# An S5 scan inside a matmul stream: two blocks encoded and two decoded in one visit of TensorE, and two of each block's sums on GpSimd

## The chip, the cores and the metric

The kernel runs on one core of a Trainium2 chip. The metric is the device time of one execution in microseconds; lower is better. The core's engines are TensorE (PE in the profile, with its weight loads as PEld), VectorE (DVE), ScalarE (ACT), GpSimd (POOL) and SyncE (SP, which here only issues DMAs). Each takes its instructions in the order in which the built program holds them, and waits on semaphores for the others.

## The reference

Two layers of a decoder trunk over 256 positions of width 2048. The first joins a Mamba-2 mixer and an attention; the second, which the change touches, is an S5 mixer: a projection to u and a gate, 128 groups of 16 channels that each drive a complex diagonal state of 64, then GELU, a GLU, the gate and an output projection.

```python
def s5_ssm(u, lam_re, lam_im, log_dt, b_re, b_im, c_re, c_im, d_skip):
    ...
    lam_bar = jnp.exp(lam * dt)
    b_bar = ((lam_bar - 1.0) / lam)[..., None] * lax.complex(b_re.astype(f32), b_im.astype(f32))
    ...
    def step(h, u_blk):
        bu = jnp.einsum('gnm,blgm->blgn', b_bar, u_blk.astype(jnp.complex64))
        bu = bu.at[:, 0].add(lam_bar * h)
        a = jnp.broadcast_to(lam_bar, bu.shape)
        _, hs = lax.associative_scan(_linear_recurrence, (a, bu), axis=1)
        y = jnp.einsum('gmn,blgn->blgm', c_mat, hs).real
        return hs[:, -1], y
    ...

def s5_mixer(x, w_in, ..., w_glu, w_out):
    u, gate = jnp.split(x @ w_in, 2, axis=-1)
    y = jax.nn.gelu(s5_ssm(u, ...))
    ga, gb = jnp.split(y @ w_glu, 2, axis=-1)
    y = ga * jax.nn.sigmoid(gb)
    return (y * jax.nn.silu(gate)) @ w_out
```

## The kernel before

**The stream of weights.** All projections are cut into units: 128x1024 blocks of weights, each loaded by SyncE into a buffer `raw` (L361), rounded by ScalarE to a high half `wh` (L367), and reduced by VectorE to the rest `wl` (L372). `wh`, `wl` and `raw` have four buffers each, and `split_to` (L328) prepares a unit three units ahead. TensorE multiplies high by high, high by low and low by high. In the products of kind x (L425) a unit is 12 matmuls of 512 columns; in the wide ones (L481, L484) it is 8 of 512 and 8 of 256.

**The scan between the units.** The second layer's scan is done in 16 blocks `b` of 8 groups, while TensorE works on the input projection's later products. `ssm(b)` defines the parts of a block: `load` brings its weights `wt` (896 KB, L1578) by a DMA of GpSimd's queue; `u_load` brings its input `um` for two blocks in four DMAs (L1558, L1559); `table` fills `rt` on GpSimd (L1585, L1586); `enc` is 16 matmuls of 64x64 into the PSUM tile `enc` (L1595); `rec1` turns that by cos and sin on VectorE, two products (L1605) and two sums (L1612, L1613); `rec2` is the recurrence itself, two scans along positions (L1620), two products that turn back (L1607) and two sums (L1622, L1623) into `gt`; `dec` is 24 matmuls of 64x64 from `gt` and `um` into the PSUM tile `dec` (L1636, L1640); `act` is a GELU on ScalarE (L1644) and four DMAs of 32 KB of ScalarE's queue (L1648, L1649). Each small matmul is two records in the profile. `y_load` brings four blocks' y back (L1662), and `y_split` cuts it in high and low halves (L1672, L1673). `wt` has four buffers, `gt`, `p1`, `p2`, `rt` and `ys` two, the PSUM tiles `enc` and `dec` one.

**What sets the order.** `at(t, f)` puts a part on step t, and the steps are a queue `back` that `pump` empties evenly over the units of seven products and eight units more. A scheduler then lays out each engine's instructions by its own timeline at build time; `tc.issue_after` ties an instruction behind another on its engine. Encode of block b stands on step 2b+1 (0 for the first), its decode on 2b+5: each visit of TensorE to the small matmuls decodes one block and encodes the block two further on. The first two visits only encode and the last two only decode, 18 visits in all.

Of the kernel before, what the change touches and what calls it, by code (L numbers as in the profile page):

```python
# [16 lines left out]
P = 128  # L17
# [6 lines left out]
HU = KT // HK  # L24
ALPHA = 4.0 ** 0.25
NKEEP = 6
NEND = 448
# [162 lines left out]
def trunk(tc, io, out):  # L190
# [8 lines left out]
    with ExitStack() as top:  # L199
# [1310 lines left out]
        with ExitStack() as l1:  # L1510
# [49 lines left out]

            steps = {}

            def at(t, f):
                steps.setdefault(t, []).append(f)

            ysd = {}

            def ssm(b):
# [4 lines left out]
                def load():  # L1573
                    wt = d["w"] = w1("wt", [P, 1792], 4)
                    with ExitStack() as pin:
                        if b:
                            pin.enter_context(tc.issue_after((after[b - 1] if b > 2 else after["u"]).ins))
                        nc.gpsimd.dma_start(wt, wb[b])  # L1578
# [9 lines left out]
                def enc():  # L1588
                    px = d["x"] = sp.tile([P, 2, 512], F32, tag="enc", name=nm("enc"))
                    wt, u = d["w"], um[b // 2]  # L1590
                    for q in range(2):
                        for r in range(2):
                            for e, i, at in tiles:
                                a = 2 * q + e
                                T.matmul(px[64 * at : 64 * at + 64, i, r * 128 + q * 64 : r * 128 + q * 64 + 64],  # L1595
                                         wt[64 * i : 64 * i + 64, a * P + 64 * r : a * P + 64 * r + 64],
                                         u[64 * i : 64 * i + 64, 4 * b2 + a, :], start=True, stop=True)

                def turned(src):
                    p1, p2 = w1("p1", [P, 2, 256]), w1("p2", [P, 2, 256])  # L1600
                    for p, t in ((p1, d["cos"]), (p2, d["sin"])):
                        if src is None:
                            t4 = t.rearrange("p r (i n) -> p r i n", i=2)
                            sv = d["x"][:, :, 0:256].rearrange("p i (r n) -> p r i n", r=2)
                            V.tensor_tensor(p.rearrange("p r (i n) -> p r i n", i=2), sv, t4, op=OP.mult)  # L1605
# [4 lines left out]
                def rec1():  # L1610
                    p1, p2 = turned(None)
                    V.tensor_tensor(p1[:, 0], p1[:, 0], p2[:, 1], op=OP.add)  # L1612
                    V.tensor_tensor(p1[:, 1], p1[:, 1], p2[:, 0], op=OP.subtract)  # L1613
                    d["p"] = p1

                def rec2():
# [5 lines left out]
                    V.tensor_tensor(gt[:, 0], p1[:, 0], p2[:, 1], op=OP.subtract)  # L1622
                    V.scalar_tensor_tensor(gt[:, 1], p1[:, 1], -1.0, p2[:, 0], op0=OP.mult, op1=OP.subtract)  # L1623

                def dec():
                    wt, u, gt = d["w"], um[b // 2], d["g"]
                    py = d["y"] = sp.tile([P, 2, 512], F32, tag="dec", name=nm("dec"))
                    for q in range(2):
                        for part in range(3):
                            for e, i, at in tiles:  # L1630
                                a = 2 * q + e
                                rows = slice(64 * at, 64 * at + 64)
                                o = py[64 * e : 64 * e + 64, at, q * 64 : q * 64 + 64]
                                if part == 0:
                                    rhs = u[rows, 8 + 2 * b2 + q, :] if e else u[rows, 4 * b2 + a, :]
                                    T.matmul(o, wt[rows, 1024 + 64 * a : 1088 + 64 * a], rhs, start=True, stop=False)  # L1636
                                else:
                                    k = 512 + 256 * (part - 1) + 64 * (2 * i + q)
                                    n = 64 * (2 * i + q)
                                    T.matmul(o[:, 1:64], wt[rows, k : k + 64], gt[rows, part - 1, n : n + 63], start=False, stop=part == 2)  # L1640

                def act():
                    ys = w1("ys", [P, 2, 2, 64])
                    A.activation(ys, d["y"][:, :, 0:128].rearrange("p i (q c) -> p i q c", c=64), AF.Gelu_apprx_tanh)  # L1644
                    dst = yd[j][16 * h : 16 * h + 16].rearrange("(i q e) a c -> e a i q c", i=2, e=2)
# [4 lines left out]

                t = 2 * b + min(b, 1)
                at(2 * b + 6, act)
                at(2 * b + 5, dec)
                at(t + 2, rec2)
                at(t + 1, rec1)
                at(t, enc)
                at(t - 1, table)
                at(t - 2, load)

# [30 lines left out]

            at(36, scanned)
            sg1 = wk.tile([P, 2, D], F32, tag="sg1", bufs=1, name="sg1")
# [263 lines left out]
```

## Time and profile before

| | |
|---|---|
| time, median of 3 runs | 1300.84 us (1300.39 to 1301.18) |
| the profiled execution: time, span | 1300.75 us, 1299.0 us |
| first encode, last decode, start | 878.3 us, 1042.4 us |
| granted TensorE clock | 0.998 of full speed, mean |

The span runs from the first to the last instruction; the 1.75 us around it are the launch. The scan lies between 878 and 1043 us. In the rows of a timeline the start comes first, then the duration, engine, line, operation and tiles; neighbours on an engine overlap at their edges, so what one costs in a full row is the distance from its start to the next start.

### The profile page before, as it was taken

What the parts mean: (1) busy time and instruction counts of PE and PEld (TensorE: products, weight loads), DVE (VectorE), ACT (ScalarE), POOL (GpSimd) and SP (SyncE); (2) the same over time, 40 slices, a digit from 0 to 9 for tenths busy, and PEclk for the clock granted to TensorE, in tenths of its full rate; (3) what the DMA queues carried; (4) which work ended last, traced back from release to release, by engine and by line L of the source; (5) the groups of instructions that cost most, each with busy time, mean ns of one, the idle gap of its engine ahead of it and who ended that gap; (6) DMA issues with size and microseconds to landing.
All of it is one profiled execution on the core that took longest, in us unless ns stands there. A gap on an engine that the chain in (4) does not pass through costs nothing.

```text
span 1299.0 us, 21556 instructions
## 1 busy us (share of the span) xinstructions
PE 1292.0 (99%) x7939; PEld 1091.1 (84%) x7939; DVE 1036.1 (80%) x1726; ACT 738.5 (57%) x1000; POOL 316.5 (24%) x617
## 2 busy tenths in 40 slices
PE   9999999999999999999999999999999999999998
PEld 9988888888888888888888888888888888888886
DVE  6678988996898887777777777858989859988665
ACT  5557668974644654554575555354345557766441
POOL 0033678888880000000000110023232001110000
PEclk9999999999999999999999999999999999999999
DMA  8556567666567667757759978479989789887762
GB/s 316 180 164 203 186 230 232 220 197 196 194 202 264 211 202 239 234 184 222 245 177 290 294 197 290 161 232 319 326 288 325 244 310 245 216 248 230 261 211 81
DMA packets 100094, 300.90 MB, mean 232 GB/s; under 512 B 19378, under 2 KB 29570, under 8 KB 99476
## 3 DMA queue, kind: packets, MB, share of 16 engines
q1 hardware_dynamic: 74356, 239.81, 54.7%
q0 software_dynamic: 11232, 46.18, 13.3%
q10 hardware_dynamic: 14400, 13.54, 3.2%
q8 instruction: 62, 1.02, 0.3%
q14 instruction: 44, 0.36, 0.1%
HBM read 276.93 MB, written 21.00 MB: 229 GB/s over the span
## 4 chain that ended last, share of the span: by engine, by line
PE 99%; DMA 1%; SPq 0%; ACT 0%; DVE 0%; issue 0%
PE main L425 54%; PE main L481 17%; PE main L484 9%; PE main L526 7%; PE main L448 3%; PE aux L631 2%; PE aux L979 1%; PE enc L1595 1%; PE aux L1085 1%; PE dec L1640 1%; PE aux L1204 1%; PE aux L1172 1%; DMA raw<-in_wi 1%; PE dec L1636 0%; PE turn L631 0%; PE aux L1171 0%
## 5 line engine op out<-in xcount | busy, mean ns | idle before, releaser
L372 DVE TENSOR_TENSOR wl<-raw,wh 128x1024 fp32r<-128x1024 f32 x400 | 493.6, 1239 | 185.0 <-ACT wh L367 176.0
L367 ACT ACTIVATE wh<-raw 128x1024 fp32r<-128x1024 f32 x400 | 421.2, 1058 | 367.0 <-PE main L425 184.4
L425 PE MATMUL main<-wh,A 128*128 128x512 f32 x1216 | 392.4, 394 | 0.0
L425 PEld LDWEIGHTS main<-wh,A 128*128 128x128 f32 x1216 | 228.0, 188 | 47.1 <-issue 0.3
L425 PE MATMUL main<-wh,C 128*128 128x512 f32 x832 | 265.2, 393 | 0.0
L425 PE MATMUL main<-wl,A 128*128 128x512 f32 x608 | 238.2, 392 | 0.0
L481 PE MATMUL main<-A,wh 128*128 128x512 f32 x768 | 199.4, 395 | 0.0
L425 PEld LDWEIGHTS main<-wh,C 128*128 128x128 f32 x832 | 155.9, 188 | 33.3
L425 PE MATMUL main<-wl,C 128*128 128x512 f32 x416 | 162.6, 391 | 0.0
L481 PEld LDWEIGHTS main<-A,wh 128*128 128x128 f32 x768 | 136.0, 189 | 23.1 <-issue 0.3
L425 PEld LDWEIGHTS main<-wl,A 128*128 128x128 f32 x608 | 114.3, 188 | 22.5
L484 PEld LDWEIGHTS main<-A,wl 128*128 128x128 f32 x768 | 108.8, 190 | 10.4
L484 PE MATMUL main<-A,wl 128*128 128x256 f32 x768 | 112.2, 282 | 0.0
L903 POOL TENSOR_TENSOR c<-c 128x8 f32<-128x8 f32 (+2 forms) x192 | 100.0, 538 | 26.5 <-DMA wb<-c 18.7
L324 POOL DMA_DIRECT2D block<-in_wo x12 | 10.4, 866 | 370.6 <-DVE wl L372 331.2
L425 PEld LDWEIGHTS main<-wl,C 128*128 128x128 f32 x416 | 78.1, 188 | 15.9
L372 DVE TENSOR_TENSOR wl<-block,wh 128x1024 fp32r<-128x1024 f32 x60 | 73.0, 1222 | 15.0 <-ACT wh L367 14.8
L367 ACT ACTIVATE wh<-block 128x1024 fp32r<-128x1024 f32 x60 | 63.0, 1059 | 36.6 <-PE main L425 21.7
L481 PE MATMUL main<-C,wh 128*128 128x512 f32 x192 | 50.4, 396 | 0.0
L905 POOL TENSOR_TENSOR c<-c,c 128x4 f32<-128x4 f32 (+2 forms) x96 | 47.5, 495 | 7.5
L906 POOL TENSOR_TENSOR c<-c,c 128x4 f32<-128x4 f32 (+2 forms) x96 | 46.5, 485 | 0.0
L324 POOL DMA_DIRECT2D block<-in_wglu x18 | 15.5, 916 | 104.3 <-DVE wl L372 87.0
(377 smaller groups left out, 1680.1 us busy)
## 6 DMA issues: line engine op xcount, KB each, us to landing
raw<-in_wi SPq DMA_DIRECT2D x270, 512.0 KB
raw<-in_wo SPq DMA_DIRECT2D x84, 512.0 KB
raw<-in_wglu SPq DMA_DIRECT2D x46, 512.0 KB
wt<-wb POOLq DMA_DIRECT2D x16, 896.0 KB, 7.4
block<-in_wglu POOLq DMA_DIRECT2D x20, 512.0 KB, 8.5
wb<-ob ACTq DMA_DIRECT2D x16, 512.0 KB
block<-in_wo POOLq DMA_DIRECT2D x12, 512.0 KB, 7.1
block<-in_wglu SPq DMA_DIRECT2D x12, 512.0 KB
```

The source lines that it names most:

```text
L324: added.append(nc.gpsimd.dma_start(blocks[g, name, k].rearrange("p k n -> p (k n)"), source[by][k], accum_op=OP.add))
L367: high = A.activation(wh, raw, AF.Copy)
L372: splits[n] = (loaded[-1], high, V.tensor_tensor(wl, raw, wh.bitcast(F32), op=OP.subtract))
L425: end = T.matmul(ps[o], l[:, k, sl], r[:, j, :], start=start and i == 0, stop=stop and i == 2, skip_group_check=free)
L448: T.matmul(pv[o // 2][:, o % 2, :], l[:, j, sl], r[:, k, :], start=first and i == 0 and o % 2 == 0, stop=end and i == 2 and o % 2 == 1, sk ...
L481: T.matmul(ps[o], wh[:, j, o * P : o * P + P], xx[:, k, :, :].rearrange("p a n -> p (a n)"), start=u + j == 0, stop=False, skip_group_chec ...
L484: lastmm[:] = [T.matmul(ps[o][:, S : 2 * S], wl[:, j, o * P : o * P + P], xh[:, k, :], start=False, stop=last and j == HK - 1, skip_group_ ...
L526: lastmm[:] = [T.matmul(ps, p, q[:, j, :], start=begin, stop=False, skip_group_check=True)]
L631: end = T.transpose(dst[:, i * P : i * P + P], s, ident)
L903: G.tensor_tensor(p[:, :, :, 0:m], cs[:, :, :, 1 : m + 1], cs[:, i, :, n : n + 1].unsqueeze(1).to_broadcast([P, 2, 4, m]), op=OP.mult)
L905: G.tensor_tensor(cs[:, 0, :, n + 1 : n + 1 + m], p0[:, 0, :, 0:m], p1[:, 1, :, 0:m], op=OP.subtract)
L906: G.tensor_tensor(cs[:, 1, :, n + 1 : n + 1 + m], p0[:, 1, :, 0:m], p1[:, 0, :, 0:m], op=OP.add)
```

## The change

Two neighbouring blocks share a visit. The list `VISIT` holds the step on which the two blocks of a pair are encoded, one after the other, into the two halves of one PSUM tile; behind them, on the same step, the two blocks of the pair before are decoded into one PSUM tile (`late_at` puts parts at the end of a step). All these matmuls are tied in one chain (`chained`), and the chain is tied in its turn behind the second block's last scan sum. The acts of both blocks stand on the step after. `rec1` and `rec2` stay by block, on steps of their own, but the two sums of `rec1` go to GpSimd. Loads, tables, `u_load`, `y_load` and `y_split` move to new steps; there are about twice as many steps over the same units.

```diff
+VISIT = [1, 12, 21, 30, 38, 46, 54, 62, 70]
...
+            behind = {}
+            psx = [None, None]
+            link = [None]
+
+            def chained(o, w, r, start, stop):
+                with ExitStack() as pin:
+                    if link[0] is not None:
+                        pin.enter_context(tc.issue_after(link[0].ins))
+                    link[0] = T.matmul(o, w, r, start=start, stop=stop)
...
+            def late_at(t, f):
+                behind.setdefault(t, []).append(f)
...
-                            pin.enter_context(tc.issue_after((after[b - 1] if b > 2 else after["u"]).ins))
+                            pin.enter_context(tc.issue_after((after[b - 1 - b2] if b > 1 else after["u"]).ins))
...
                 def enc():
-                    px = d["x"] = sp.tile([P, 2, 512], F32, tag="enc", name=nm("enc"))
+                    if b2 == 0:
+                        psx[0] = sp.tile([P, 2, 512], F32, tag="enc", name=nm("enc"))
+                    px = d["x"] = psx[0]
...
-                                T.matmul(px[64 * at : 64 * at + 64, i, r * 128 + q * 64 : r * 128 + q * 64 + 64],
...
+                                n = 256 * b2 + r * 128 + q * 64
+                                chained(px[64 * at : 64 * at + 64, i, n : n + 64],
...
                 def rec1():
                     p1, p2 = turned(None)
-                    V.tensor_tensor(p1[:, 0], p1[:, 0], p2[:, 1], op=OP.add)
-                    V.tensor_tensor(p1[:, 1], p1[:, 1], p2[:, 0], op=OP.subtract)
+                    G.tensor_tensor(p1[:, 0], p1[:, 0], p2[:, 1], op=OP.add)
+                    G.tensor_tensor(p1[:, 1], p1[:, 1], p2[:, 0], op=OP.subtract)
...
-                    V.scalar_tensor_tensor(gt[:, 1], p1[:, 1], -1.0, p2[:, 0], op0=OP.mult, op1=OP.subtract)
+                    done = V.scalar_tensor_tensor(gt[:, 1], p1[:, 1], -1.0, p2[:, 0], op0=OP.mult, op1=OP.subtract)
+                    if b2:
+                        link[0] = done
...
                 def dec():
-                    py = d["y"] = sp.tile([P, 2, 512], F32, tag="dec", name=nm("dec"))
+                    if b2 == 0:
+                        psx[1] = sp.tile([P, 2, 512], F32, tag="dec", name=nm("dec"))
+                    py = d["y"] = psx[1]
...
-                t = 2 * b + min(b, 1)
-                at(2 * b + 6, act)
-                at(2 * b + 5, dec)
-                at(t + 2, rec2)
-                at(t + 1, rec1)
+                t = VISIT[b // 2]
+                at(VISIT[b // 2 + 1] + 1, act)
+                late_at(VISIT[b // 2 + 1], dec)
                 at(t, enc)
-                at(t - 1, table)
-                at(t - 2, load)
+                late_at(t + b2, rec1)
+                at(t + 2 + b2, rec2)
+                at(t - 2, table)
+                at(t - 6 + b2, load)
...
-                    at(2 * b + min(b, 1) - 2, lambda b=b: u_load(b // 2))
+                    at(VISIT[b // 2] - 6, lambda b=b: u_load(b // 2))
...
-                    at(2 * b + 8, lambda b=b: y_load(b // 4))
+                    at(4 * b + 16 if b < 15 else 76, lambda b=b: y_load(b // 4))
                     if b < 15:
-                        at(2 * b + 11, lambda b=b: y_split(b // 4))
+                        at(4 * b + 22, lambda b=b: y_split(b // 4))
+            for t, fs in behind.items():
+                steps.setdefault(t, []).extend(fs)
...
-            at(36, scanned)
+            at(75, scanned)
```

What the built program makes of it, engine by engine. The lines of the changed kernel are higher by one up to L1571 (the matmul in `chained`, which stands for encode and decode alike); its sums of `rec1` on GpSimd are L1628 and L1629, its `rec2` L1636 to L1639, its loads L1591, its act L1664 to L1669. The number behind a name tells buffers apart.

TensorE before, one visit (block 11 is decoded, block 13 encoded), between two main matmuls:

```order
L425 MATMUL main_10412<-wh_10562,C_8570 128x512
L1636 MATMUL dec_10704<-um_10249,wt_10374 64x64 x4
L1640 MATMUL dec_10704<-gt_10607,wt_10374 64x63 x8
L1636 MATMUL dec_10704<-um_10249,wt_10374 64x64 x4
L1640 MATMUL dec_10704<-gt_10607,wt_10374 64x63 x8
L1595 MATMUL enc_10738<-um_10504,wt_10633 64x64 x16
L425 MATMUL main_10762<-wh_10637,C_8570 128x512
```

TensorE in the change, its sixth visit (pair 5, blocks 10 and 11, is encoded, and pair 4 decoded):

```order
L426 MATMUL main_10349<-wh_10261,C_8570 128x512
L1571 MATMUL enc_10370<-um_10288,wt_10286 64x64 x16
L1571 MATMUL enc_10370<-um_10288,wt_10320 64x64 x16
L1571 MATMUL dec_10403<-um_10014,wt_10012 64x64 x4
L1571 MATMUL dec_10403<-gt_10277,wt_10012 64x63 x8
L1571 MATMUL dec_10403<-um_10014,wt_10012 64x64 x4
L1571 MATMUL dec_10403<-gt_10277,wt_10012 64x63 x8
L1571 MATMUL dec_10403<-um_10014,wt_10046 64x64 x4
L1571 MATMUL dec_10403<-gt_10311,wt_10046 64x63 x8
L1571 MATMUL dec_10403<-um_10014,wt_10046 64x64 x4
L1571 MATMUL dec_10403<-gt_10311,wt_10046 64x63 x8
L426 MATMUL main_10348<-wh_10295,C_8570 128x512
```

Both blocks of a pair now stand in one group, encodes first. All visits but the second look so; the second is cut in three by main matmuls (the encodes and the first four decode matmuls; then the even block's `gt`; then, a unit on, the odd block's). With the first, which only encodes, and the ninth, which only decodes, there are 11 groups. Between visits stand 3, 7, 7, 7, 5, 7, 6 and 6 units; before, three.

ScalarE in the change, behind the eighth visit:

```order
L368 ACTIVATE wh_10982<-raw_10980 128x1024
L1664 ACTIVATE ys_10998<-dec_10925 128x256
L1664 ACTIVATE ys_11004<-dec_10925 128x256
L1668 DMA yd_8807<-ys_10998 64x2x64
L1669 DMA yd_8807<-ys_10998 64x2x64
L1668 DMA yd_8807<-ys_10998 64x2x64
L1669 DMA yd_8807<-ys_10998 64x2x64
L1668 DMA yd_8807<-ys_11004 64x2x64
L1669 DMA yd_8807<-ys_11004 64x2x64
L1668 DMA yd_8807<-ys_11004 64x2x64
L1669 DMA yd_8807<-ys_11004 64x2x64
L368 ACTIVATE wh_11018<-raw_11016 128x1024
```

Before, one `ys` and four DMAs stood between two rows of `wh`; now two and eight. VectorE in the change, at the same visit:

```order
L373 TENSOR_TENSOR wl_10984<-raw_10980,wh_10982 128x1024
L1621 TENSOR_TENSOR p_1733_10974<-enc_10892,wt_10794 128x512
L1621 TENSOR_TENSOR p_1734_10975<-enc_10892,wt_10794 128x512
L1621 TENSOR_TENSOR p_1740_11010<-enc_10892,wt_10846 128x512
L1621 TENSOR_TENSOR p_1741_11011<-enc_10892,wt_10846 128x512
L373 TENSOR_TENSOR wl_11020<-raw_11016,wh_11018 128x1024
L1636 SCALAR_TENSOR_TENSOR gt_11034<-rt_10868,p_1733_10974 128x256 x2
L373 TENSOR_TENSOR wl_11052<-raw_11048,wh_11050 128x1024
L1623 TENSOR_TENSOR p_1746_11037<-gt_11034,wt_10794 128x512
```

The rows of `rec1` of both blocks come together, then a `wl` of the `wh` that stands behind the eight DMAs (11018), and only then the scans. Up to the odd block's last sum (gt_11068) there stand four `wl` and one `y_split` in this round; the rounds up to the sixth, seventh and eighth visits hold three, five (and a `y_split`) and four.

GpSimd in the change, after the fifth visit, with the weights of pair 5:

```order
L1628 TENSOR_TENSOR p_1616_10217<-p_1616_10217,p_1617_10218 128x256
L1629 TENSOR_TENSOR p_1616_10217<-p_1616_10217,p_1617_10218 128x256
L1628 TENSOR_TENSOR p_1623_10253<-p_1623_10253,p_1624_10254 128x256
L1629 TENSOR_TENSOR p_1623_10253<-p_1623_10253,p_1624_10254 128x256
L1591 DMA wt_10286<-wb_84 128x1792
L1559 DMA um_10541<-ud_8803 64x8x64
L1560 DMA um_10541<-ud_8803 64x4x64
L1559 DMA um_10541<-ud_8803 64x8x64
L1560 DMA um_10541<-ud_8803 64x4x64
L1591 DMA wt_10320<-wb_85 128x1792
```

Before, the loads of the two blocks stood apart, each on a step of its own and behind no sums; here both stand behind the four sums of the pair just encoded, and the second behind the `um` of the next pair too. VectorE's order has the three splits of the next units ahead of the products that these sums read.

More of the change, by code (lines that the diff above doesn't have):

```diff
@@ L1594, in enc @@
                                 a = 2 * q + e
-                                T.matmul(px[64 * at : 64 * at + 64, i, r * 128 + q * 64 : r * 128 + q * 64 + 64],
-                                         wt[64 * i : 64 * i + 64, a * P + 64 * r : a * P + 64 * r + 64],
-                                         u[64 * i : 64 * i + 64, 4 * b2 + a, :], start=True, stop=True)
+                                n = 256 * b2 + r * 128 + q * 64
+                                chained(px[64 * at : 64 * at + 64, i, n : n + 64],
+                                        wt[64 * i : 64 * i + 64, a * P + 64 * r : a * P + 64 * r + 64],
+                                        u[64 * i : 64 * i + 64, 4 * b2 + a, :], True, True)
                 def turned(src):
@@ L1603, in turned @@
                             t4 = t.rearrange("p r (i n) -> p r i n", i=2)
-                            sv = d["x"][:, :, 0:256].rearrange("p i (r n) -> p r i n", r=2)
+                            sv = d["x"][:, :, 256 * b2 : 256 * b2 + 256].rearrange("p i (r n) -> p r i n", r=2)
                             V.tensor_tensor(p.rearrange("p r (i n) -> p r i n", i=2), sv, t4, op=OP.mult)
@@ L1632, in dec @@
                                 rows = slice(64 * at, 64 * at + 64)
-                                o = py[64 * e : 64 * e + 64, at, q * 64 : q * 64 + 64]
+                                o = py[64 * e : 64 * e + 64, at, 128 * b2 + q * 64 : 128 * b2 + q * 64 + 64]
                                 if part == 0:
                                     rhs = u[rows, 8 + 2 * b2 + q, :] if e else u[rows, 4 * b2 + a, :]
-                                    T.matmul(o, wt[rows, 1024 + 64 * a : 1088 + 64 * a], rhs, start=True, stop=False)
+                                    chained(o, wt[rows, 1024 + 64 * a : 1088 + 64 * a], rhs, True, False)
                                 else:
@@ L1639, in dec @@
                                     n = 64 * (2 * i + q)
-                                    T.matmul(o[:, 1:64], wt[rows, k : k + 64], gt[rows, part - 1, n : n + 63], start=False, stop=part == 2)
+                                    chained(o[:, 1:64], wt[rows, k : k + 64], gt[rows, part - 1, n : n + 63], False, part == 2)
                 def act():
                     ys = w1("ys", [P, 2, 2, 64])
-                    A.activation(ys, d["y"][:, :, 0:128].rearrange("p i (q c) -> p i q c", c=64), AF.Gelu_apprx_tanh)
+                    A.activation(ys, d["y"][:, :, 128 * b2 : 128 * b2 + 128].rearrange("p i (q c) -> p i q c", c=64), AF.Gelu_apprx_tanh)
                     dst = yd[j][16 * h : 16 * h + 16].rearrange("(i q e) a c -> e a i q c", i=2, e=2)
```

## The prediction

> **What bounds the kernel now.** I read the page's busy times first, then its chain that ended last, then the stretch in which the scan runs.
>
> ```profile
> PE 1292.0 (99%) x7939; PEld 1091.1 (84%) x7939; DVE 1036.1 (80%) x1726; ACT 738.5 (57%) x1000; POOL 316.5 (24%) x617
> PE 99%; DMA 1%; SPq 0%; ACT 0%; DVE 0%; issue 0%
> 894.50:1042.00 147.50, 147.50 (x1773) 122.24 (x1776) 133.89 (x204) 72.70 (x90) 33.98 (x65) 1.00 0.88 292
> ```
>
> The third line is the table of busy time by stretch: microseconds, then PE, its weight loads, DVE, ACT, POOL, the granted clock (1.00), the share of DMA and GB/s. TensorE is busy in all 147.50 us from the first decode to the last; VectorE is at 133.89, or 91%. So the time is the sum of what TensorE is given, and an edit counts in two ways only: what it takes out of TensorE's own row, and any wait it puts in. The waits of the other engines say how thick the cover is (who waited for whom, 878 to 1045 us: total, times, longest; TensorE has no line there).
>
> ```profile
> DVE wl L372 <- ACT wh L367: 13.8, 12, 2.8
> ACT wh L367 <- DMA yd<-ys: 10.2, 3, 3.4
> ```
>
> VectorE waits for ScalarE's high halves, and ScalarE's high halves wait behind its own four DMA issues of y.
>
> **What a visit costs.** The timeline of TensorE, one visit with decode and encode, and the last, with decode alone (start, duration, count):
>
> ```profile
> 963.35 0.62 PE L425 MATMUL main<-wh,C 128*128 128x512 f32 x2
> 963.80 0.39 PE L425 MATMUL main<-wl,C 128*128 128x512 f32 x1
> 964.03 0.39 PE L425 MATMUL main<-wh,C 128*128 128x512 f32 x1
> ...
> 965.67 0.50 PE L425 MATMUL main<-wh,C 128*128 128x512 f32 x1
> 966.01 0.39 PE L425 MATMUL main<-wl,C 128*128 128x512 f32 x1
> 966.24 0.62 PE L425 MATMUL main<-wh,C 128*128 128x512 f32 x2
> ...
> 1041.35 0.39 PE L425 MATMUL main<-wh,A 128*128 128x512 f32 x1
> ...
> 1042.18 0.41 PE L1640 MATMUL dec<-gt,wt 64*64 64x63 f32 x16
> 1042.52 0.50 PE L425 MATMUL main<-wh,A 128*128 128x512 f32 x1
> 1042.86 0.40 PE L425 MATMUL main<-wl,A 128*128 128x512 f32 x1
> 1043.10 0.39 PE L425 MATMUL main<-wh,A 128*128 128x512 f32 x1
> ```
>
> Three main matmuls take 964.03 - 963.35 = 0.68, so 0.227 each, and a unit of twelve 2.72. From the last main before the visit to the third after it: 966.24 - 964.03 = 2.21, less 0.68, is 1.53 for 80 records (40 matmuls in two passes); the second visit: 1.75 - 0.68 = 1.07 for 48. The 32 of the encode thus cost 0.46, or 0.0144 each, and 1.07 - 48 x 0.0144 = 0.38 is fixed: what it costs to go over to the small tiles and back.
>
> **The sum, part by part.** The 16 x 80 small records stay. Before there are 18 visits; in the change's order there are 11 groups, since the second visit is cut in three. Saved: 7 x 0.38 = 2.7 us, with nothing beside it, as TensorE is the bound.
>
> The rest is what could make TensorE wait. Nothing in the trace shows such a wait, so I chain it from rows. First ScalarE, the act of one block:
>
> ```profile
> L1644 ACT ACTIVATE ys<-dec x16: 365/376/387, 898.7 to 1042.7; 128x256 f32<-128x256 f32 x16
> 965.41 0.37 ACT L1644 ACTIVATE ys<-dec 128x256 f32<-128x256 f32 x1
> 965.81 0.60 ACTq L1648 DMA_DIRECT2D yd<-ys  x1
> 966.45 0.62 ACTq L1649 DMA_DIRECT2D yd<-ys  x1
> 967.11 1.32 ACTq L1648 DMA_DIRECT2D yd<-ys  x1
> 968.47 0.62 ACTq L1649 DMA_DIRECT2D yd<-ys  x1
> 969.19 1.06 ACT L367 ACTIVATE wh<-raw 128x1024 fp32r<-128x1024 f32 x1 [3.41 <-DMA yd<-ys]
> ```
>
> Four issues take 3.28 here, with one long one; without it, 4 x 0.66 = 2.64. In the change both blocks' ys, then all eight issues, stand ahead of the next wh: 2 x 0.40 + 6.0 (between 5.3 and 6.6, as about every second block has a long issue) + 1.06 = 7.9 us from the end of the decode until the next wl can start. Each handover adds about 0.1 (decode ends 1042.18 + 0.41 = 1042.59, its ys starts 1042.7); with three of them I add 0.3. Then VectorE:
>
> ```profile
> 965.43 1.27 DVE L1620 TENSOR_TENSOR_SCAN gt<-rt,p 128x256 f32<-128x256 f32 x2
> 966.73 1.49 DVE L1607 TENSOR_TENSOR p<-gt,wt 128x512 f32<-128x512 f32 x2
> 968.14 1.21 DVE L372 TENSOR_TENSOR wl<-raw,wh 128x1024 fp32r<-128x1024 f32 x1
> 969.28 0.41 DVE L1622 TENSOR_TENSOR gt<-p,p 128x256 f32<-128x256 f32 x1
> 969.61 0.41 DVE L1623 SCALAR_TENSOR_TENSOR gt<-p,p 128x256 f32<-128x256 f32 x1
> 969.95 1.28 DVE L1605 TENSOR_TENSOR p<-enc,wt 128x512 f32<-128x512 f32 x2
> 971.26 0.42 DVE L1612 TENSOR_TENSOR p<-p,p 128x256 f32<-128x256 f32 x1
> L1673 DVE TENSOR_TENSOR A<-ut,A 128x512 fp32r<-128x512 f32 x8 | 5.5, 710 | 0.9 <-ACT A L1672 0.9
> ```
>
> From start to start: a split wl 1.14, two scans 1.30, two turning products 1.41, two last sums 0.67, so rec2 of a block 3.38 and of a pair 6.8; the products of rec1 1.31. The sums of rec1 go to GpSimd: 0.34 each, 1.3 us a pair, leaves VectorE. But the order puts a wl between rec1 and the scans, and this wl needs the wh behind the eight issues. VectorE stands idle until then, and only after it come all of rec2 and the splits. From the end of one decode to the odd block's gt, which the next decode reads:
>
> - chain: 7.9 + 0.3 + m x 1.14 + 6.8 + s, with m the splits ahead of that gt in VectorE's order and s = 1.2 where a y_split stands among them (two at 0.71, overlapping);
> - TensorE: n x 2.72 + 0.38 + 64 x 0.0144 of encode + 48 x 0.0144 of the even decode = n x 2.72 + 1.99, and 1.07 at the last, which has no encode.
>
> The order gives n and m. Visits 3 and 4 to the next have n = 7: 21.0 of TensorE against 20.8 or less, no wait. Visit 7 (n 7, m 5, s): 21.9 against 21.0, waits 0.9. Visit 8 (n 6, m 4): 19.6 against 18.3, waits 1.2. Visit 9 (n 6, m 4, s): 20.8 against 17.4, waits 3.3. Visit 6 comes after only 5 units: 18.4 against 15.6, 2.8 by this chain; it has another, of weights:
>
> ```profile
> L1578 POOL DMA_DIRECT2D wt<-wb x16: 528/555/563, 847.9 to 1005.4; - x16
> DMA to landing us min/median/max: 4.8/7.4/13.2
> 945.87 0.82 POOL L1586 COPY rt<-rho 128x252 f32<-128x252 f32 x1
> 947.08 0.71 POOL L1558 DMA_DIRECT2D um<-ud  x1 [0.39 <-issue]
> ...
> 949.71 0.56 POOL L1578 DMA_DIRECT2D wt<-wb  x1
> 955.59 0.40 POOL L1586 COPY rt<-rho 128x252 f32<-128x252 f32 x1
> L750 POOL TENSOR_TENSOR ew<-ew x5: 725/734/1557, 98.8 to 107.4; 32x256 f32<-32x256 f32 x5
> ```
>
> With four buffers and two blocks a visit, wt of pair 5 is loaded only after the decode of pair 3, and GpSimd's order puts it behind the four moved sums. From the odd gt of visit 5: three splits 3.4, four products 2.6, two sums 1.5 (0.73 each, the nearest row, of 32 partitions; the even sums lie under the odd products), one wt 0.55, four um 2.63 (947.08 to 949.71), the second wt 7.4: 18.1, against TensorE's 0.69 + 0.38 + 13.6 + 0.46 = 15.1. Wait 3.0, which holds the 2.8 as well.
>
> The second visit's decode of the even block, 3 units after the first encode, meets its gt within a few tenths, and after visit 3 a split comes late by about as much; I put 0.5 on each, between 0 and 1.1. Sum of the waits: 3.0 + 0.9 + 1.2 + 3.3 + 1.0 = 9.4; less 2.7 is +6.7. Against the profiled execution's own 1300.75 that is 1307.4, and against the median of 1300.84, which is 0.09 above it, 1307.5.
>
> The low end of the terms (5.3 for the issues, wt landing in 4.8, the halves 0): visits 6 to 9 wait 2.1, 0.2, 0.5, 2.6, less 2.7: +2.7, 1303.5. The high end: wt landing in 13.2 at visit 6 adds 5.8, issues at 6.6 add 0.6 to three visits, sums that take 1.557 add 1.6: with all of them together +16, or 1317, so I end the range just below, at 1316. Loads, tables and y_load in other steps, and the first encode some three units later, cost nothing of their own: GpSimd has 34 us of work in 147.5, and what its order delays is the wt above.
>
> A rule that speaks against the move of the sums: the rows show a copy on GpSimd at 0.40 and at 0.82 where it fell between two products of VectorE, the pair of which took 1.41 from start to start. [...]
>
> **Rivals.** *Faster: the splits come in time.* If the wl ahead of the scans waited no longer than the wh's that wait now (3.4 at the longest), TensorE would lose nothing and the time would be 1300.84 - 2.7 = 1298.1. For it: TensorE has no wait in this stage now, with VectorE at 91%, and 1.3 us of each pair leaves VectorE. Against it: it decides at 4.6 us from decode to wl (7.9 less visit 9's 3.3), which eight issues of 0.62 alone exceed. Chance 0.12.
>
> *No change that can be measured.* The waits are there, but at the low end of every term or below it, and eat the gain: between 1298.3 and 1303.4. Chance 0.16.
>
> [...] Chance 0.08.
>
> **How the numbers follow.** A measurement of this kernel can tell about 0.2%, 2.6 us, from no change. The forecast, waits at visits 6 to 9 over the saving, has 0.64 and its own range is 1303.5 to 1312. Faster by more than 0.2% is the first rival alone, 0.12; within, 0.16; slower, 0.64 + 0.08 = 0.72. From 1299.5 to 1316 all but about 0.15 is held: most of the first rival below, the end of the port above.
>
> **What would show it.** In the changed kernel's trace: 11 groups of small matmuls, 0.38 saved on each of 7; TensorE, which has no wait in the stage now, waiting on dec L1571 for gt, longest at the last visit, and on enc at the sixth for wt; VectorE idle some 4 us in each visit ahead of a wl, released by ScalarE after eight DMA issues in a row; GpSimd's sums near 0.73 while VectorE is idle. Wrong would be: eight issues that take under 4 us, a wh that runs before them, or wt landing so late (over 10 us) that the encodes of several visits wait.

## The result: 1.4% slower, and slower than the range allowed

The changed kernel takes 1319.18 us (median of four runs, 1317.57 to 1319.51), the kernel before beside it 1301.01: the ratio is 1.0136, with a 95% interval of 1.0124 to 1.0148. The sign was forecast, and the places of most waits; the time lies 11.7 us above the forecast of 1307.5, and above the range, which ended at 1316.

The page of the profiled run (1317.57 us, span 1315.8, so 16.8 above the span of before), busy times and the chain that ended last:

```profile
PE 1296.0 (98%) x7939; PEld 1095.3 (83%) x7939; DVE 1026.0 (78%) x1694; ACT 736.8 (56%) x1000; POOL 345.1 (26%) x649
PE 89%; DVE 4%; DMA 3%; issue 1%; ACT 1%; ACTq 1%; POOL 0%; DVEq 0%; POOLq 0%
```

Before, the chain was 99% PE. Now a tenth of it lies on other engines: TensorE waits. Its own list of waits, 860 to 1110 us (total, times, longest):

```profile
PE dec L1571 <- DVE gt L1638: 8.1, 4, 4.0
PE enc L1571 <- DMA wt<-wb: 4.0, 1, 4.0
PE dec L1571 <- issue: 0.5, 1, 0.5
PE main L426 <- DVE wl L373: 0.2, 1, 0.2
```

That is 12.8 us where there was none: by the timeline 4.0 at visit 2, 0.5 at visit 4, 4.0 at visit 6 (the wt), 0.3, 1.2 and 2.7 at visits 7, 8 and 9. The waits behind them, 878 to 1085 us:

```profile
DVE wl L373 <- ACT wh L368: 55.7, 20, 7.1
ACT wh L368 <- DMA yd<-ys: 44.0, 7, 7.0
ACT wh L368 <- DMA raw<-in_wi: 32.0, 13, 4.2
```

VectorE's waits for ScalarE had been 13.8 in 12, with 2.8 the longest. The second line is the eight issues in a row; one such row of ScalarE (the first is at 972.75):

```profile
972.75 0.60 ACTq L1668 DMA_DIRECT2D yd<-ys  x1
...
976.20 0.62 ACTq L1669 DMA_DIRECT2D yd<-ys  x1
978.00 0.58 ACTq L1668 DMA_DIRECT2D yd<-ys  x1
979.25 0.58 ACTq L1669 DMA_DIRECT2D yd<-ys  x1
979.94 2.01 ACT L368 ACTIVATE wh<-raw 128x1024 fp32r<-128x1024 f32 x2 [6.94 <-DMA yd<-ys]
```

Six issues at 0.6 to 0.8, then two that stand 1.8 and 1.25 behind the one before. From the first issue to the end of the eighth it is 5.4 to 7.1 us in the eight visits, 6.6 in the mean.

The third line is ScalarE waiting for raw weights. Four of these waits, 1.7 to 2.9 us each, stand before visit 2, where the kernel before has none. GpSimd, ScalarE, VectorE and TensorE there:

```profile
876.58 0.69 POOL L1559 DMA_DIRECT2D um<-ud  x1 [2.17 <-DMA wt<-wb]
880.66 0.63 POOL L1560 DMA_DIRECT2D um<-ud  x1 [3.38 <-DMA wt<-wb]
...
887.14 1.06 ACT L368 ACTIVATE wh<-raw 128x1024 fp32r<-128x1024 f32 x1 [2.64 <-DMA raw<-in_wi]
...
888.24 1.23 DVE L373 TENSOR_TENSOR wl<-raw,wh 128x1024 fp32r<-128x1024 f32 x1 [2.47 <-ACT wh L368]
889.38 2.48 DVE L1621 TENSOR_TENSOR p<-enc,wt 128x512 f32<-128x512 f32 x4
...
900.67 0.79 PE L1571 MATMUL dec<-gt,wt 64*64 64x63 f32 x16 [3.96 <-DVE gt L1638]
```

Three wt loads (2.7 MB) stand ahead of um on GpSimd's queue, and um and the raw tiles come late. The first encode starts at 885.56 instead of 878.30; that is its place in the order, TensorE does not wait ahead of it. Its products stand behind a late wl, from there on VectorE is full (busy in all 11.29 us from 889.38 to the decode; the odd block's products and three wl stand ahead of the even block's gt), and the decode, 15 us after the encode, waits 3.96 for gt.

Last, a term that the prediction does not have at all: the granted clock. Stretches of 3.41 us of the changed kernel (behind the length stands PE's busy time; the column before the last two is the granted clock): each odd row holds one of the three longest waits, each even one is what follows.

```profile
897.69:901.10 3.41, 0.43 (x12) 0.30 (x16) 3.41 (x7) 0.00 (x0) 0.31 (x1) 1.00 0.49 161
901.10:904.51 3.41, 3.41 (x47) 3.04 (x48) 3.38 (x6) 0.15 (x1) 1.44 (x3) 0.50 0.62 174
986.44:989.85 3.41, 0.10 (x4) 0.10 (x8) 3.41 (x6) 0.00 (x0) 2.74 (x3) 1.00 0.99 397
989.85:993.26 3.41, 3.41 (x128) 3.35 (x128) 3.41 (x6) 2.34 (x2) 3.41 (x3) 0.50 0.90 308
1054.70:1058.11 3.41, 1.34 (x42) 1.10 (x43) 3.41 (x6) 1.06 (x2) 0.00 (x0) 1.00 0.48 141
1058.11:1061.52 3.41, 3.41 (x10) 2.65 (x9) 1.21 (x2) 0.42 (x2) 0.00 (x0) 0.50 0.85 256
```

After each, the granted clock is 0.50 for 3.41 us; three main matmuls take 1.28 there (1059.30 to 1060.58) and 0.69 behind it (1061.71 to 1062.40). By my estimate from the 0.50, 1.7 us of work is done in each: 3 x 1.7 = 5.1 lost. The account of the span is then 12.8 + 5.1 - 2.7 saved = 15.2 of 16.8; the rest is in pieces that I do not name.

### The profile page after: what moved, and what is told of

Same layout as the page of the kernel before. It is cut to its first block, busy times and chain, and to the rows that moved or that the text cites. A ratio compares the mean times of both kernels' runs of the same rounds, so it can differ in the third digit from the quotient of the medians.

```text
span 1315.8 us, 21535 instructions
## 1 busy us (share of the span) xinstructions
PE 1296.0 (98%) x7939; PEld 1095.3 (83%) x7939; DVE 1026.0 (78%) x1694; ACT 736.8 (56%) x1000; POOL 345.1 (26%) x649
## 4 chain that ended last, share of the span: by engine, by line
PE 89%; DVE 4%; DMA 3%; issue 1%; ACT 1%; ACTq 1%; POOL 0%; DVEq 0%; POOLq 0%
PE main L426 47%; PE main L482 16%; PE main L485 8%; PE main L527 7%; PE main L449 3%; DMA raw<-in_wi 2%; PE aux L632 2%; DVE wl L373 1%; DVE gt L1636 1%; DMA wt<-wb 1%; DVE p L1623 1%; PE aux L980 1%; PE aux L1086 1%; ACT wh L368 1%; PE dec L1571 1%
## 5 line engine op out<-in xcount | busy, mean ns | idle before, releaser
L485 PEld LDWEIGHTS main<-A,wl 128*128 128x128 f32 x768 | 108.8, 190 | 10.4
L904 POOL TENSOR_TENSOR c<-c 128x8 f32<-128x8 f32 (+2 forms) x192 | 104.8, 563 | 27.9 <-DMA wb<-c 20.2
L325 POOL DMA_DIRECT2D block<-in_wo x12 | 10.4, 866 | 370.6 <-DMA raw<-in_wo 327.7
L426 PEld LDWEIGHTS main<-wl,C 128*128 128x128 f32 x416 | 78.1, 188 | 16.8 <-DVE wl L373 0.6
L906 POOL TENSOR_TENSOR c<-c,c 128x4 f32<-128x4 f32 (+2 forms) x96 | 44.9, 468 | 7.5
L907 POOL TENSOR_TENSOR c<-c,c 128x4 f32<-128x4 f32 (+2 forms) x96 | 43.5, 453 | 0.0
```

Source lines behind the costliest of these rows:

```text
L325: added.append(nc.gpsimd.dma_start(blocks[g, name, k].rearrange("p k n -> p (k n)"), source[by][k], accum_op=OP.add))
L426: end = T.matmul(ps[o], l[:, k, sl], r[:, j, :], start=start and i == 0, stop=stop and i == 2, skip_group_check=free)
L485: lastmm[:] = [T.matmul(ps[o][:, S : 2 * S], wl[:, j, o * P : o * P + P], xh[:, k, :], start=False, stop=last and j == HK - 1, skip_group_ ...
L904: G.tensor_tensor(p[:, :, :, 0:m], cs[:, :, :, 1 : m + 1], cs[:, i, :, n : n + 1].unsqueeze(1).to_broadcast([P, 2, 4, m]), op=OP.mult)
L906: G.tensor_tensor(cs[:, 0, :, n + 1 : n + 1 + m], p0[:, 0, :, 0:m], p1[:, 1, :, 0:m], op=OP.subtract)
L907: G.tensor_tensor(cs[:, 1, :, n + 1 : n + 1 + m], p0[:, 1, :, 0:m], p1[:, 0, :, 0:m], op=OP.add)
```

## The experiments

**Theories.** 1: each visit waits by a chain of its own, the eight issues (4, 7, 8, 9), the wt loads of the start (2), the wt of the next pair (6), and a long wait (2.7 to 4.0 us in the three above) costs half clock on top. 2, a rival: the sums on GpSimd hold up VectorE. 3, another: the clock falls for some other reason. Theories 5 and 6 came from the first four runs and are named where they appear. Ratios are against the kernel before on the same chip.

### One cure at a time

**The acts apart.**

```diff
-                at(VISIT[b // 2 + 1] + 1, act)
+                at(VISIT[b // 2 + 1] + 1 + 2 * b2, act)
```

> The odd block's act (its ys and four of the eight DMA issues) stands two steps behind the even block's, instead of in the same step. Theory 1 (each visit's wait comes from its own chain: eight issues, wh, wl, the scans, gt; and a wait of 2.9 us or more costs a further 1.7 us at half clock): the waits at visits 4, 7, 8 and 9 (0.7, 0.6, 1.5, 3.0) and the spell after visit 9 go, part comes back where the second four issues hold up a later wh; waits of visits 2 and 6 stay: about 1312 us, between 1309 and 1315. Theory 2 (GpSimd's sums hold up VectorE): the sums are untouched, 1319.

Measured: 1309.59 us, 1.0065 (1.0052 to 1.0078), 9.6 less than the change. The groups of four issues take 2.6 to 3.3 us, VectorE's waits for wh fall to 35.8 us, longest 4.4. Visits 8 and 9 wait no more; 3.5 at visit 2 stays, visits 5 and 7 wait 1.7 and 1.2. Theory 1 holds for the eight issues. It missed visit 6, whose wait for wt it left standing: that wait is gone too, and in this run 6 units lie between visits 5 and 6 instead of 5. So not all of the 9.6 us is due to the issues. Theory 2 cannot give the gain, since the sums are where they were.

**The first wt loads later.**

```diff
-                            pin.enter_context(tc.issue_after((after[b - 1 - b2] if b > 1 else after["u"]).ins))
+                            pin.enter_context(tc.issue_after((after[b - 1 - b2] if b > 3 else after["um"]).ins))
```

(`after["um"]` is the last um load.)

> The wt loads of blocks 1 to 3 stand behind the um loads of the first pair in GpSimd's order instead of ahead of them. Theory 1 says that visit 2's wait of 4.0 us comes from those loads: um is issued later and the raw tiles of the weights come late to ScalarE. So the wait falls to about 1 and the half-clock spell after it goes: 1319.2 - 3 - 1.7 = 1314.5 us, between 1312.5 and 1317. Theory 2 (GpSimd's sums hold up VectorE): 1319.

Measured: 1314.17 us, 1.0105 (1.0090 to 1.0121), 5.0 less. The first encode is back at 877.7, ScalarE waits for no raw tile before visit 2, and visit 2 waits 0.2 instead of 4.0. As expected; but visit 8 now waits 2.6 instead of 1.2, and two main matmuls wait 2.6 together for a wl. The edit brings both the encodes and the raw tiles forward, so it does not say how much of the 4.0 is due to each.

**The sums back on VectorE.**

```diff
-                    G.tensor_tensor(p1[:, 0], p1[:, 0], p2[:, 1], op=OP.add)
-                    G.tensor_tensor(p1[:, 1], p1[:, 1], p2[:, 0], op=OP.subtract)
+                    V.tensor_tensor(p1[:, 0], p1[:, 0], p2[:, 1], op=OP.add)
+                    V.tensor_tensor(p1[:, 1], p1[:, 1], p2[:, 0], op=OP.subtract)
```

> The two sums of rec1 are back on VectorE. Theory 1: VectorE does them while it would wait for a wl, so visits 7 to 9 wait as before; at visit 6 the sums leave GpSimd's way to the second wt (4.2 us becomes about 2.7, so that spell may go too), and at visit 2 the sums of the odd block no longer stand behind um's issues: 1316 us, between 1313 and 1319. [...]

Measured: 1344.36 us, 1.0336 (1.0321 to 1.0350), 25 us more than the change: theory 1 missed by 28 us, and theory 2, under which most of the 18 us would go, by more. ScalarE's and GpSimd's rows at visit 5 of this kernel, and the first line of TensorE's waits:

```profile
983.65 0.60 ACTq L1668 DMA_DIRECT2D yd<-ys  x1
...
987.47 0.58 ACTq L1668 DMA_DIRECT2D yd<-ys  x1
991.92 0.58 ACTq L1669 DMA_DIRECT2D yd<-ys  x1
995.69 0.58 ACTq L1668 DMA_DIRECT2D yd<-ys  x1
998.86 0.58 ACTq L1669 DMA_DIRECT2D yd<-ys  x1
999.54 2.95 ACT L368 ACTIVATE wh<-raw 128x1024 fp32r<-128x1024 f32 x3 [15.53 <-DMA yd<-ys]
```

```profile
982.75 0.55 POOL L1591 DMA_DIRECT2D wt<-wb  x1 [8.04 <-PE dec L1571]
...
985.95 0.56 POOL L1591 DMA_DIRECT2D wt<-wb  x1
```

```profile
PE main L426 <- ACT wh L368: 18.8, 5, 6.4
```

The eight issues take 15.8 us: the last three come 3.2 to 4.5 us apart. GpSimd, which has no sums to do, has put out 2.2 MB of wt and um in the first 4 us of them. In the changed kernel its sums stood between, and the same load went out at 977.56, when six of the eight issues were through. This made theory 5: **ScalarE is held by its own DMA issues when too many of them meet GpSimd's loads**, and the sums on GpSimd had been a cover. It is drawn from the times of the issues alone; no trace shows what holds an issue. Its rival, theory 6: 10.6 us more work on VectorE is the loss. (The granted clock falls too: 0.989 in the mean of this run, 0.994 in the change.)

**TensorE kept busy in two waits.**

(`busy` puts n matmuls into the chain whose result nobody reads.)

```diff
...
+            def busy(o, n):
+                for _ in range(n):
+                    chained(o, idle[:, 0:1].to_broadcast([P, P]), idle.unsqueeze(1).to_broadcast([P, 4, 64]), False, True, True)
...
+                    if b == 11:
+                        busy(px[:, 0, 256:512], 26)
...
+                            if q == 0 and part == 1 and b == 15:
+                                busy(psx[1][:, 0, 256:512], 16)
```

> Idle 128x256 matmuls into unused columns stand in two of the waits: 26 (about 3.0 us) between the two encodes of visit 6, 16 (about 1.9 us) in the decode of visit 9. Nothing waits for less. Theory 1: TensorE's own pause is what halves the clock afterwards, so the two spells after visits 6 and 9 go and 2 x 1.7 us with them: 1315.8 us, between 1314.8 and 1317. Theory 3 (the clock falls for another reason, or the pause is not what counts): 1319, or a few tenths above.

Measured: 1318.89 us, 1.0137 (1.0123 to 1.0151). The clock behaved as theory 1 said, after visits 6 and 9 it is 1.00 (the last three columns are the granted clock, the DMA share and GB/s):

```profile
992.00:996.00 4.00, 4.00 (x30) 3.30 (x27) 4.00 (x6) 0.66 (x2) 3.28 (x5) 1.00 0.82 239
1056.00:1060.00 4.00, 4.00 (x56) 3.24 (x55) 4.00 (x5) 1.04 (x3) 0.00 (x0) 1.00 0.55 192
```

and the time is the same. Visit 7 starts 1.0 us sooner (1011.66, not 1012.63), and TensorE waits more behind it; here two rows of this kernel, and below them the row of the changed kernel that answers to the second:

```profile
1015.79 0.39 PE L426 MATMUL main<-wl,C 128*128 128x512 f32 x1 [1.15 <-issue]
...
1035.55 0.68 PE L1571 MATMUL dec<-gt,wt 64*64 64x63 f32 x16 [1.48 <-DVE gt L1644]
```

```profile
1035.55 0.68 PE L1571 MATMUL dec<-gt,wt 64*64 64x63 f32 x16 [1.17 <-DVE gt L1638]
```

The decode of visit 8 starts at 1035.55 in both. Full clock cannot get TensorE past a gt that ScalarE and VectorE finish when they finish. So theory 3 is out: behind the two pauses the clock was 0.50, and without them it is 1.00. But as a cost, the spell after visit 6 was free, and theory 1's price for it, 1.7 us, was wrong. For the spell after visit 9 the run says less: in its profiled execution the clock after visit 2, where nothing was put in, is 0.50 from 900 to 906 us at least, where the change has 3.41 us of it, so that at most 4.2 us less stand at half clock in all, and not 6.8.

### Theory 5 against theory 6

**The acts apart and the sums back on VectorE** (the first and the third edit):

> The sums back on VectorE, and the odd block's act two steps later. Theory 5, made from the run with the sums back (its eight issues took 6.7 to 15.8 us instead of 5.4 to 7.1, since GpSimd, free of the sums, issued the wt and um loads at the same time): groups of four issues don't fill the queue, so the loss goes: about 1311 us, between 1308 and 1316. Theory 6 (32 sums at 0.33, 10.6 us on a VectorE that is full): 1320 or more.

Measured: 1307.51 us, 1.0051 (1.0039 to 1.0063). The same sums that went with 25 us more beside eight issues go with 2.1 less beside four. Theory 6 is out.

**The sums on GpSimd, but behind the loads.**

```diff
+                        if b + 3 - b2 in got:
+                            pin.enter_context(tc.issue_after(got[b + 3 - b2].ins))
                         G.tensor_tensor(p1[:, 0], p1[:, 0], p2[:, 1], op=OP.add)
...
+                if 1 < b < 14 and not b2:
+                    late_at(t, lambda: [pend[b + 2](), pend[b + 3]()])
```

(`got` holds the wt loads, `pend` the functions that issue them.)

> The sums stay on GpSimd, but from the second pair on the two wt loads and the um loads of the next pair stand ahead of the four sums in its order. Theory 5: the loads now meet the eight issues of y, which take 10 to 16 us a visit instead of 5.4 to 7.1: 1340 us, between 1330 and 1350. Theory 6 (only the work on VectorE counts, loads ahead of time are good): visit 6's wait of 4.2 us for wt goes, 1315 us or less.

Measured: 1345.01 us, 1.0337 (1.0324 to 1.0351), with VectorE's work that of the change. Issues at visit 6 of this kernel:

```profile
1011.16 0.58 ACTq L1673 DMA_DIRECT2D yd<-ys  x1
...
1024.13 0.58 ACTq L1674 DMA_DIRECT2D yd<-ys  x1
1024.82 2.01 ACT L368 ACTIVATE wh<-raw 128x1024 fp32r<-128x1024 f32 x2 [13.41 <-DMA yd<-ys]
```

They take 13.6 us here, 13.0 at visit 4, and 5.2 to 9.3 at the others. Moving the loads alone costs what moving the sums did, and TensorE now waits 9.7 us for wh, for which it did not wait in the change: that the issues take longer where the loads go out beside them is shown. How much of the 26 us this makes is not: the sums now stand behind loads that wait for the decode, which can make gt late as well (14.7 us of waits instead of 8.1), and the mean granted clock is 0.987 instead of 0.994.

**The two cures of visits together** (acts apart, first wt loads later):

> Both edits together: the odd block's act two steps later, and the first wt loads behind um. Theory 1: the two cures act on different visits and add up: 1319.2 - 9.6 - 5.0 = 1304.6 us, between 1303 and 1308. If VectorE and ScalarE are full in this stage, so that a wait that goes comes back at the next visit, less adds up: 1308 to 1310.

Measured: 1310.71 us, 1.0068 (1.0049 to 1.0087), single runs from 1303.4 to 1311.6. They do not add up: in the profiled run the wait of visit 2 for gt is gone and one of 4.8 us for wt stands at visit 4. The alternative in the text was right in kind; its range ended at 1310.

**Those two, and the loads ahead of the sums:**

> Three edits: the act apart, the first wt loads behind um, and from the second pair on the wt and um loads ahead of the four sums. Theory 5: four issues at a time don't fill the queue, and the encodes no longer wait for wt (1.4 us in the run with the act apart): 1303 us, between 1301 and 1306. If four issues stall on the loads as well: above 1310.

Measured: 1307.61 us, 1.0051 (1.0037 to 1.0064). No encode waits longer than 0.6 us for wt, as theory 5 said, but groups of four issues now take up to 7.6 us. So four issues, too, came further apart beside the loads; neither expectation was right in its number.

### Fewer issues, and one part alone

**One ys and four issues a pair.**

```diff
-                    ys = w1("ys", [P, 2, 2, 64])
-                    A.activation(ys, d["y"][:, :, 128 * b2 : 128 * b2 + 128]...
+                    ys = w1("ys", [P, 2, 4, 64], 1)
+                    A.activation(ys, d["y"][:, :, 0:256]...
...
-                at(VISIT[b // 2 + 1] + 1, act)
+                if b2:
+                    at(VISIT[b // 2 + 1] + 1, act)
```

> Both blocks' decodes are taken out of PSUM by one ys instruction, and go out in four DMA issues of 64 KB instead of eight of 32 KB; TensorE's and GpSimd's orders stay word for word (but for three main matmuls). Theory 5, by the number of issues: 0.6 + 2.6 + 1.1 = 4.3 us from the decode to the next wh's end instead of 7.9 or more, so the waits at visits 4, 7, 8 and 9 go: about 1308.5 us, between 1306 and 1311. If ScalarE is held by the bytes under way and not by the number of issues, four take as long as eight: 1319.

Measured: 1312.04 us, 1.0085 (1.0071 to 1.0099). A group of ScalarE's issues, and TensorE's waits:

```profile
993.23 0.60 ACT L1664 ACTIVATE ys<-dec 128x512 f32<-128x512 f32 x1 [2.87 <-PE dec L1571]
993.86 0.60 ACTq L1667 DMA_DIRECT2D yd<-ys  x1
...
995.83 0.73 ACTq L1668 DMA_DIRECT2D yd<-ys  x1
996.68 1.06 ACT L368 ACTIVATE wh<-raw 128x1024 fp32r<-128x1024 f32 x1 [2.85 <-PE main L426]
```

```profile
PE dec L1571 <- DVE gt L1638: 4.6, 1, 4.6
PE enc L1571 <- DMA wt<-wb: 3.5, 1, 3.5
```

The same 256 KB in four issues take 2.7 to 3.5 us instead of 5.4 to 7.1; here the number of issues is what counts, not the bytes. ScalarE's waits for its own issues are gone from its list. The waits at visits 4, 7, 8 and 9 are gone, the time is 7.1 us less, and what is left is visits 2 and 6 (4.6 and 3.5 us, where the change has 4.0 and 4.0). The time ends 1 us above the range given.

**The same, with the first wt loads later:**

> One ys and four issues a pair, and the first wt loads behind um. Theory 1 for visit 2, theory 5 for the rest: 1308.5 less 4 to 5: 1304 us, between 1301 and 1307. If a wait that goes comes back at the next visit, as it did with the two cures before: 1307 to 1310.

Measured: 1308.83 us, 1.0063 (1.0049 to 1.0077): 3.2 less. Visit 2 waits no more; visit 6 still waits 4.1 for wt, and visit 4 1.6.

**The same again, with the wt loads ahead of the sums:**

> One ys and four issues a pair, the first wt loads behind um, and from the second pair on the wt and um loads ahead of the four sums. Theory 5 by number: no encode waits for wt, no wh waits long: 1301 us, between 1298.5 and 1305. By bytes: the loads hold up the issues as they did with eight, 1320 or more.

Measured: 1308.60 us, 1.0062 (1.0050 to 1.0075), a miss: the wait for wt has moved from visit 6 to visit 3 (3.7 us), and the issues, 2.6 to 4.8, are not held much.

**The kernel before with the sums of rec1 on GpSimd, one part of the change alone:**

> The kernel before, with only the two sums of rec1 moved to GpSimd: one part of the change alone. Theory 5: the sums take 0.73 instead of 0.33 on a way with five units of room, nothing waits: 1301 us, between 1299.5 and 1302.5. Theory 2 (sums beside VectorE hold it up): 1305 or more.

Measured: 1301.10 us, 1.0002 (0.9993 to 1.0010). The sums in that kernel (minimum, median, maximum in ns):

```profile
L1612 POOL TENSOR_TENSOR p<-p,p x16: 723/732/1588, 880.6 to 1029.8; 128x256 f32<-128x256 f32 x16
L1613 POOL TENSOR_TENSOR p<-p,p x16: 727/1221/1715, 881.3 to 1031.4; 128x256 f32<-128x256 f32 x16
```

They take 0.72 to 1.72 us, and the time does not move, with TensorE busy throughout (195.00 us of 870 to 1065). Theory 2 is out as the cause of the 18 us. In the paired order moving the sums back gains 2.1 us (beside four issues, above) and 4.0 (below); no run tells what part of that is VectorE being held up, and what part GpSimd's loads coming late.

### Visit 6, and whether a paired order can win

**Two empty steps in the changed kernel,** so that visit 6 comes 7 units after visit 5 instead of 5:

```diff
+            for t in (42, 58):
+                at(t, lambda: None)
```

> The changed kernel with two empty steps in the list, after the fifth and the seventh visit, so that the sixth comes 7 units after the fifth instead of 5 (and the fifth 6 after the fourth instead of 7). Theory: visit 6's wait is one of position; it falls from 4.2 us to 1 or less, while earlier visits come a little sooner: about 1316 us, between 1313.5 and 1318. If the load's own time or GpSimd's order sets it, the wait moves with the visit: 1319.

Measured: 1318.88 us, 1.0139 (1.0126 to 1.0152). Visit 6's wait is gone and others took its place: 0.9 for wt and 1.4 for gt at visit 5, 1.1 at visit 3, 3.3 at visit 9. Alone it is worth nothing.

**Two empty steps on top of one ys a pair and the first wt loads later:**

> One ys and four issues a pair, the first wt loads behind um, and the two empty steps. Without them it waited 4.3 us at visit 6 with 2 x 1.7 us of half clock behind. Theory: both go, and the fifth visit, a unit earlier, gets about 1.5: 1308.8 - 4.3 - 3.4 + 1.5 = 1302.6 us, between 1300.5 and 1305. If the wait moves with the visit: 1307 to 1310.

Measured: 1305.84 us, 1.0035 (1.0023 to 1.0047), 3.0 less than without the steps: neither the 1302.6 of the theory nor unchanged. Visit 6's wait is gone, 1.8 for wt stands at visit 5, and the mean granted clock is 0.999.

**And the sums back on VectorE:**

> As the run before in this set, with the sums of rec1 on VectorE, so that GpSimd issues the loads of wt at once after each decode. If the four sums ahead of wt are what makes it late, no encode waits: 1301 us, between 1299 and 1304. If the loads, coming at once, hold up even four issues of y (they took up to 8.4 us in the run with the act apart and the sums back): 1305 or more.

Measured: 1301.85 us, 1.0010 (1.0001 to 1.0018; twelve runs, 1299.67 to 1306.29). With the sums gone from GpSimd the loads go out with the decode, and four issues stand it (2.6 to 4.7 us): 4.0 us less, where beside eight the same edit cost 25. In its profiled run, the longest of the twelve, visit 5 waits 3.4 us for wt, which stood behind a read of yd on GpSimd's queue.

**That read behind the wt loads** (and, with it, the first two `y_load` and `y_split` on later steps and four more empty steps; the units between the visits stay as they were):

```diff
+                    if j < 2:
+                        pin.enter_context(tc.issue_after(got[4 * j + 9].ins))
                     tail["y"] = nc.gpsimd.dma_start(y5[j], yd[j]...
```

> As the paired kernel with the sums on VectorE and the two empty steps; the two reads of yd that stood ahead of a pair's wt loads on GpSimd's queue stand behind them (and their splits one step later). If the read is what held the wt back: the fifth visit's wait goes, 1299 us, between 1298 and 1301, which is the 2.7 us of seven groups less, less a residue. If the loads themselves take too long beside the others: 1301 to 1303.

Measured: 1301.91 us, 1.0008 (0.9998 to 1.0018; twelve runs). The wait for wt is gone, and the time stays with the run before it. The page's busy times of this run, and TensorE's waits:

```profile
PE 1289.0 (99%) x7939; PEld 1090.7 (84%) x7939; DVE 1031.7 (79%) x1726; ACT 737.8 (57%) x992; POOL 327.5 (25%) x617
PE main L426 <- issue: 1.1, 1, 1.1
PE dec L1571 <- DVE gt L1639: 0.8, 1, 0.8
PE dec L1571 <- issue: 0.5, 1, 0.5
```

TensorE is busy 3.0 us less than before (1289.0 for 1292.0): the gain of the pairing is there. But it stands idle 3.4 us more in return (span less busy time is 10.4 instead of 7.0), 2.4 of it in these three waits. No version beat the kernel before.

**The ladder.** From the change, one edit after the other: 1319.2; one ys and four issues 1312.0; first wt loads later 1308.8; empty steps 1305.8; sums back on VectorE 1301.9. Steps of 7.1, 3.2, 3.0 and 4.0: the order counts, since the last one ahead of the first costs 25 us.

## Why the prediction was wrong in size

- **The saving** was right: 0.38 a group. The changed kernel has the 11 groups of the forecast, but its waits and spells hide the 2.7 us. The last version, whose second visit is whole and whose first is cut in two, has 10 groups, and its TensorE is busy 3.0 us less, which is 8 x 0.38.
- **The eight issues** were right as a cause and a little small in size: 6.0 (5.3 to 6.6) forecast, 5.4 to 7.1 measured, above 6.6 in five of the eight visits. Taking four of them out gives 7.1 us, spreading them 9.6. That they can take 16 was not seen. I priced them by rows of four issues, beside which GpSimd's queue sends out one wt and one pair's um at most (1.3 MB, 986.25 to 989.43 us before), and did not ask what it sends out beside eight.
- **The sums on GpSimd** were right in price (0.73 for 0.73). In the changed kernel half of them took 0.73, and the longest, 1.73 at 908.16, lies beside a wl and scans of VectorE; in the kernel before with the sums moved they stretch to 1.72. The last rival, the port, with 0.08 in the sum of the chances, is a term that no run shows; what the runs show in its place is that the sums alone on GpSimd give 1.0002.
- **Visits 6 to 9:** 3.0, 0.9, 1.2 and 3.3 forecast, 4.0, 0.3, 1.2 and 2.7 measured. The mechanisms were the named ones, as the runs with the acts apart and with four issues show for 7 to 9. That the sizes came so near is partly luck: at visit 9 the wl came 8.55 us after the decode, where the sum has 8.2, and the way from there to the gt took 11.6, where it has 12.6. At visit 6 the position counts: two empty steps take the wait away, and on the changed kernel it then turns up elsewhere.
- **The step that failed** is "a few tenths" at visit 2, 0.5 in the sum, 4.0 measured. It took the first encode's later start as costing nothing ("Loads, tables and y_load in other steps ... cost nothing of their own"). I looked at what GpSimd's order delays on GpSimd, and not at what the loads do to the raw tiles of ScalarE, nor at how much VectorE has to do between that encode and the decode. The run with those loads later shows the price, 5.0 us: its 1314.2 lies inside the range. Which share is the raw tiles' and which the encode's place stays open.
- **The half clock** has no term in the sum. By the estimate above it makes 5.1 of the 10.1 us that the sum is short in the profiled run; the rest is 3.5 at visit 2, 1.0 at visit 6, less 1.2 at the other visits, and 1.7 unnamed. But as a cause it is weak: with the spells after visits 6 and 9 taken away the time stayed. I take this to be the sum's other assumption failing too. It treats each visit alone, as if VectorE and ScalarE started each chain with nothing left over; in the changed kernel the chain through them sets the pace, and a wait cured at one visit comes back at another (the empty steps alone, the two cures together).
- **"Faster" and "no change"** would have needed the wl to wait under 4.6 us after the decode. With one ys and four issues the way from the ys behind the decode to the end of the wh is 4.5 (993.23 to 996.68 + 1.06 in that run's rows), and there visits 7 to 9 wait no more: the point of decision agrees with that.

What stays open: why single runs of some of the cured kernels differ by 6 to 8 us (1303.4 to 1311.6, 1299.7 to 1306.3) where those of before lie within 2.6 but for one. The mean granted clock of these runs differs too (0.994 to 0.997 in the first kernel, 0.995 to 0.999 in the second), but no run separates that from the transfers.

## What to carry to other kernels

Count DMA issues as work of the engine that issues them, and look at what other queues send out in the same microseconds: eight in a row cost 5.4 to 7.1 us here, and up to 15.8 beside 2.2 MB of another queue's loads. Before moving work off an engine, ask what its new place on the other queue lets out earlier or holds back; here the sums were a cover for ScalarE. When several chains fill the same stage, a wait that is cured moves on, so cure them together, and judge a cure by the time and not by the wait that it removes.

## What the runs showed of the hardware that was not expected

**Issues that come further apart.** An issue of 32 KB mostly takes 0.58 to 0.65 us. In the changed kernel the first five or six of a visit mostly go at about that pace; then, in five of the eight visits, one or two stand 1.2 to 1.8 us behind the one before. In the run with the sums back, where wt and um of 2.2 MB go out in the same microseconds, the last three of visit 5 stand 3.2 to 4.5 us apart: 15.8 us of ScalarE's time for eight. With 64 KB an issue, four went in 2.7 to 3.5 in the first run that had them.

**Half clock behind a wait.** The three spells of the changed kernel begin at 901.10, 989.85 and 1058.11 us and last 3.41 each, at a granted clock of 0.50. They begin 88.75 and 68.26 apart, which is 26 and 20 times 3.41 to within 0.1. The length of a wait alone does not tell here whether one follows: 2.7 us at visit 9 of the change were followed by half clock (1.34 busy in the 3.41 us before it, above), while in the run with the first wt loads later a wait of 3.6 us was not (1.58 and 1.62 busy in the two stretches of 3.41 us that it lies in):

```profile
980.79:984.20 3.41, 1.58 (x37) 1.01 (x35) 3.41 (x7) 2.08 (x3) 0.90 (x3) 1.00 0.96 332
984.20:987.61 3.41, 1.62 (x108) 1.62 (x112) 3.41 (x7) 0.93 (x1) 3.41 (x1) 1.00 1.04 389
987.61:991.02 3.41, 3.41 (x46) 2.85 (x38) 3.41 (x5) 2.07 (x4) 2.69 (x4) 1.00 0.84 290
```

It may count how a wait falls on stretches of 3.41 us: that is an estimate of mine from these rows and the two distances, and no run tests it.
